# Banded attention heads as a pipeline in one fixed order, with smaller edits at the experts' start and end

## Chip, cores and metric

The kernel runs on one core of a Trainium2 chip. Its time is the device time of one execution, in microseconds (us). The program computes one layer of a diffusion backbone in one launch.

## What is computed

The reference, cut to the parts that the change touches:

```python
# banded heads: 8 query heads, 2 key/value heads, 512 tokens in 4 blocks of 128, 256 context tokens
s_loc = einsum('bnqkgd,bnjkd->bnkgqj', qbk, kband)     # own block and its neighbours
s_ctx = einsum('bnqkgd,bjkd->bnkgqj', qbk, k_ctx)
s_loc = where(|distance| <= 128 and in range, s_loc, -1e30)
p = softmax(concatenate([s_loc, s_ctx, sink_col], -1))  # sink_col: one learned number per head
o = einsum(p_loc, vband) + einsum(p_ctx, v_ctx)
x = x + g1 * (concatenate([ya, yb], -1) @ w_out)        # ya: four differential heads, yb: banded heads
hx2 = modulate(rmsnorm(x, norm2_g), sh2, sc2)
# 32 experts, each token goes to its top 4: h = xb @ w_gu[e] + b; clamped SwiGLU; a @ w_dn[e] + b
x = x + g2 * moe(hx2)
return rmsnorm(x, final_g)
```

## The kernel before

All products run on TensorE (PE). A float32 matrix is split into a high and a low part, and a product of two such matrices is three products (mm3). The stages in time are: the adaLN vectors, norms and projections; four differential heads (A); sixteen units of banded heads (B); the router; 31 experts' gate-up and down products as a pipeline; the last expert and the final norm.

A unit of the banded stage is a pair (n, m) of a block of 128 queries and a pair of heads; the loop at line 1171 goes over n and within it over m, 0 to 3. For each unit, scores_B (line 809) multiplies the queries of both heads with the keys: 512 keys where n is 0 or 3 and 640 where it is 1 or 2, cut in pieces of at most 512 columns. A piece is two products: the first on 128 rows (queries high and low against the high keys) and the second on the 64 rows of the low keys; then come masks of 128 columns. Both heads' scores lie in one PSUM tile "sc" of 1536 columns, the second from column 768. The first unit has two tiles of its own. One element per head is the sink, copied behind the scores by DVE for one head and by ACT for the other. DVE then takes both maxima (nmB), ACT both exponentials (pB, with their sums rsB), DVE the reciprocal, and DVE scales one head's pB and ACT the other's.

turn_B (870) transposes pB in groups of two key blocks for both heads (tiles "tp"), ACT copies them out as pTh and DVE takes the rest, pTl. mix_B (881) multiplies with the values into the tile "o", shared by two units. put_B (888), at odd m, adds the halves of o (yB, two copies on ACT and two adds on DVE) and splits the sum. out_proj (1040) does six products of 512 columns for one of eight row blocks of w_out; prep_out splits a part of w_out. Between units of block n stand the steps of block n - 1: norm2 (1057) at m = 0, route_T at 1, route at 2 (choice of the experts), rank at 3 (places in the experts' tables, with four indirect DMAs from POOL). router_vectors runs once.

The order of the work on each engine is a scheduler's, except where the list "pinned" names the engine: there instructions stay in the order of the program (the wrapper class at line 42, whose line 52 is the line of most rows). The banded stage isn't pinned. From line 1320 and in the experts' pipeline (1640) PE, DVE and ACT are.

In the experts' pipeline each unit is one block of 1024 weight columns or rows: unit_split (1565) splits it on ACT and DVE six units ahead of unit_products (1574). The list extra holds further steps by unit number: tables (1608) loads the four slot tables by DMAs on ACT's queue at unit 11, enter_rows adds them at unit 14. The last expert stands outside: down of expert 30 (1535), gate_up_last (1501), then its down product by the list "esq" and rows (1743), which puts results in place through the tiles p0, p1, y, h and tpm.

Of the kernel before, what the change touches and what calls it, by code (L numbers as in the profile page):

```python
# [10 lines left out]
F32 = mybir.dt.float32  # L11
# [14 lines left out]
KB = 8  # L26
# [11 lines left out]
def tile_block(ctx: ExitStack, tc: tile.TileContext, a: dict, out: bass.AP, dbg=None):  # L38
# [770 lines left out]
    def scores_B(n, m):  # L809

        b0, b1 = max(n - 1, 0), min(n + 2, 4)
        L = (b1 - b0) * 128
        nk = C + L
        g = m // 2
        rw = slice(g * 64, g * 64 + 64)
        q = qT[n]
        own = n + m < KN["own"]
        if own:
            assert nk == 512
            sv = [ps_pj() for _ in range(2)]  # L820
        else:
            s = sc_tile(KN["sB"])
            sv = [s[:, 0:TA], s[:, TA:2 * TA]]
        for i in range(2):
            hd, s = 2 * m + i, sv[i]
# [15 lines left out]
        nm = bp.tile([128, 2], F32, name="nmB", bufs=4)  # L841
        rs = bp.tile([128, 2], F32, name="rsB", bufs=4)
        w = nk if own else nk + 1
        for i in range(0 if own or KN["snk"] == "P" else 2):
            (V.tensor_copy if KN["snk"][i] == "V" else S.copy)(sv[i][:, nk:w], sinkB[:, 2 * m + i:2 * m + i + 1])
        for i in range(2):
            V.tensor_reduce(nm[:, i:i + 1], sv[i][:, 0:w], axis=AX.X, op=OP.max, negate=True)
        if own:
            es = bp.tile([128, 3, 2], F32, name="esB", bufs=1)
            V.tensor_scalar_mul(es[:, 0], sinkB[:, 2 * m:2 * m + 2], -1.0)  # L850
            V.tensor_tensor(nm, nm, es[:, 0], op=OP.min)
            V.tensor_add(es[:, 1], nm, sinkB[:, 2 * m:2 * m + 2])
            S.activation(es[:, 2], es[:, 1], AF.Exp)
        pp = []
        for i in range(2):
# [3 lines left out]
        if own:  # L859
            V.tensor_add(rs, rs, es[:, 2])  # L860
        V.reciprocal(rs, rs)
        for i in range(2):
            if KN["scB"][i] == "S":
                S.activation(pp[i][:, 0:nk], pp[i][:, 0:nk], AF.Copy, scale=rs[:, i:i + 1])
            else:
# [305 lines left out]
    for i, (n, m) in enumerate(units):  # L1171
# [4 lines left out]
        if m == 0 and n > 0:  # L1176
            start_Y(n)
# [674 lines left out]
```

## Time and profile before

| | |
|---|---|
| median of 3 runs | 1696.1 us (1688.65 to 1696.68) |
| the profiled execution | 1695.95 us, span 1694.2 us |
| TensorE's granted clock, mean | 0.965 |
| PE busy | 1609.1 us, 95% |
| DVE, ACT, POOL busy | 1482.8, 1093.7, 211.6 us |
| chain that ended last | PE 86%, DVE 5%, issue 4%, ACT 2%, DMA 2% |

Engines: PE is TensorE's products, PEld its weight loads, DVE VectorE, ACT ScalarE, POOL GpSimd, SP SyncE. PEclk is the granted clock, 1.00 or 0.50 at a time (2.4 or 1.2 GHz). A timeline row gives the start, the time that the instruction or its group took, and in brackets how long the engine had been idle and what released it.

### The profile page before, as it was taken

The numbers are of one execution on the slowest core, as the hardware profiler recorded it, in microseconds if no ns is written. First come the engines' busy times: TensorE is split into PE (matmuls) and PEld (weight loads), VectorE is DVE, ScalarE is ACT, GpSimd is POOL, SyncE is SP. The second block draws the span as 40 slices with busy tenths as digits, with TensorE's granted clock in tenths as the row PEclk, the third lists the DMA queues.
The fourth block names the chain that finished last, engine by engine and source line by source line (L and its number), as shares of the span: only waits on it lengthen the run. The fifth ranks groups of instructions, "written<-read, shape, count | busy, mean of one in ns | idle before, by whom it ended". The sixth has DMA issues, their size and how long they took to land.

```text
span 1694.2 us, 20948 instructions
## 1 busy us (share of the span) xinstructions
PE 1609.1 (95%) x7464; PEld 1286.3 (76%) x7464; DVE 1482.8 (88%) x1755; ACT 1093.7 (65%) x1406; POOL 211.6 (12%) x134
## 2 busy tenths in 40 slices
PE   7799997999888999999999999999999999999995
PEld 2687775677676888888888888888888888888873
DVE  6988797556777999999999999999999999999895
ACT  6544435445555776777776777776777776777763
POOL 0000001012331111111111111111111111111011
PEclk9999997788979999999999999999999999999998
DMA  9524325611569999999999999999999999999982
GB/s 350 174 85 131 107 88 162 169 49 40 193 234 345 352 359 367 362 361 379 376 362 364 366 365 378 382 363 367 366 363 381 374 362 367 361 369 365 363 274 91
DMA packets 115922, 494.11 MB, mean 292 GB/s; under 512 B 16641, under 2 KB 39338, under 8 KB 68642
## 3 DMA queue, kind: packets, MB, share of 16 engines
q1 hardware_dynamic: 99090, 456.44, 70.6%
q0 software_dynamic: 14128, 28.91, 8.2%
q10 hardware_dynamic: 2592, 7.34, 1.2%
q8 instruction: 61, 1.00, 0.2%
q14 instruction: 51, 0.42, 0.1%
HBM read 472.91 MB, written 27.57 MB: 295 GB/s over the span
## 4 chain that ended last, share of the span: by engine, by line
PE 86%; DVE 5%; issue 4%; ACT 2%; DMA 2%; POOL 0%; ACTq 0%; SPq 0%; DVEq 0%; POOLq 0%
PE h L52 41%; PE y L52 21%; PE pj L52 10%; PE sc L52 5%; PE tpm L52 3%; PE tp L52 3%; PE o L52 2%; DVE wp L52 1%; DVE two L52 1%; DMA ys<-slot_d 1%; PE g L52 1%; DMA w<-in_w_mod_dram 1%; PE p L52 0%; ACT wp L52 0%; ACT pB L52 0%
## 5 line engine op out<-in xcount | busy, mean ns | idle before, releaser
L52 PE MATMUL h<-two 128*128 128x512 f32 x1666 | 415.1, 400 | 1.4 <-DVE two L52 1.4
L52 PEld LDWEIGHTS h<-two 128*128 128x128 f32 x1666 | 310.1, 189 | 72.1 <-DVE two L52 2.2
L52 PE MATMUL h<-wp,two 128*128 128x512 f32 x1314 | 328.5, 400 | 4.1 <-DVE pk L52 4.1
L52 DVE TENSOR_TENSOR two<-wp,two 128x1024 fp32r<-128x1024 f32 x254 | 301.1, 1219 | 8.0 <-ACT two L52 7.9
L52 PEld LDWEIGHTS h<-wp,two 128*128 128x128 f32 x1314 | 244.4, 190 | 57.4 <-ACT two L52 4.3
L52 ACT CAST two<-wp 128x1024 fp32r<-128x1024 f32 x254 | 257.8, 1049 | 16.4 <-PE y L52 13.1
L52 DVE TENSOR_TENSOR wp<-wp 128x1024 fp32r<-128x1024 f32 x176 | 205.4, 1218 | 2.7 <-ACT wp L52 2.7
L52 DVE TENSOR_TENSOR two<-w,two 128x1024 fp32r<-128x1024 f32 x170 | 200.1, 1218 | 2.3 <-ACT two L52 2.3
L52 POOL DMA_INDIRECT acc<-ys,slot_i x31 | 103.7, 3345 | 705.4 <-DVE ys L52 705.4
L52 ACT CAST wp<-wp 128x1024 fp32r<-128x1024 f32 x176 | 176.1, 1050 | 12.8 <-PE y L52 7.7
L52 ACT CAST two<-w 128x1024 fp32r<-128x1024 f32 x170 | 170.4, 1049 | 16.6 <-PE y L52 11.9
L52 PE MATMUL y<-two,ah 128*128 128x512 f32 x540 | 169.4, 395 | 0.0
L52 PE MATMUL y<-wp,ah 128*128 128x512 f32 x452 | 142.8, 397 | 0.0
L52 DVE TENSOR_TENSOR wp<-w,wp 128x1024 fp32r<-128x1024 f32 x104 | 125.5, 1218 | 7.2 <-ACT wp L52 7.1
L52 ACT CAST wp<-w 128x1024 fp32r<-128x1024 f32 x104 | 108.8, 1049 | 27.6 <-PE pj L52 10.3
L52 PEld LDWEIGHTS y<-two,ah 128*128 128x128 f32 x540 | 101.3, 188 | 24.4
L52 ACT CAST ah<-tpm 128x512 fp32r<-128x512 f32 x64 | 37.5, 588 | 127.3 <-PE tpm L52 127.3
L52 PE MATMUL y<-two,al 128*128 128x512 f32 x270 | 106.7, 395 | 0.0
L52 PEld LDWEIGHTS y<-wp,ah 128*128 128x128 f32 x452 | 85.8, 190 | 20.7 <-ACT ah L52 0.4
L52 DVE TENSOR_TENSOR wp<-wchunk,wp 128x1024 fp32r<-128x1024 f32 x82 | 98.3, 1218 | 0.0
L52 PE MATMUL pj<-xh,wp 128*128 128x512 f32 (+1 forms) x320 | 91.7, 364 | 1.9 <-ACT xf L52 1.0
L52 PE MATMUL y<-wp,al 128*128 128x512 f32 x226 | 90.0, 398 | 2.1 <-DVE al L52 2.1
(343 smaller groups left out, 2401.0 us busy)
## 6 DMA issues: line engine op xcount, KB each, us to landing
wp<-in_w_gate_up_dram SPq DMA_DIRECT2D x139, 1024.0 KB
w<-in_w_gate_up_dram SPq DMA_DIRECT2D x87, 1024.0 KB
wp<-in_w_down_dram SPq DMA_DIRECT2D x76, 1024.0 KB
w<-in_w_down_dram SPq DMA_DIRECT2D x41, 1024.0 KB
wchunk<-in_w_gate_up_dram SPq DMA_DIRECT2D x30, 1024.0 KB
wm<-in_w_mod_dram SPq DMA_DIRECT2D x64, 256.0 KB
wchunk<-in_w_down_dram SPq DMA_DIRECT2D x11, 1024.0 KB
w<-in_w_in_dram SPq DMA_DIRECT2D x14, 512.0 KB
```

The costliest lines, as they stand in the source:

```text
L52: i = f(*args, **kwargs)
```

## The change

The function scores_B becomes a class, Scores, with one call per head for the scores and the maximum and one for the exponential. The loop's instructions on PE, DVE and ACT stay in program order, in which the next unit's two heads stand between this unit's transposes. The probabilities are no longer scaled: put_B multiplies the finished sums by the reciprocals, which PE transposes. The sink element is written by a product on PE. The low keys are copied to tiles of 128 rows, the other 64 of them zero. The slot tables are loaded at unit 4 instead of 11, two of them by GpSimd's queue, and added at unit 16 instead of 14 by one reduction. The last expert's two halves and the down product of expert 30 are units of the pipeline. Some buffers are shared or made fewer (pB 5 to 4, lg 2 to 1, fill and zt in one). In the tail, p0 and p1 become halves of the tile y, and two of the tiles of rows halves of h.

The diff, cut:

```diff
+    klB = bp.tile([128, 2, TA], F32R, name="klB")
+    for g in range(2):
+        rw, ro = slice(g * 64, g * 64 + 64), slice(64 - g * 64, 128 - g * 64)
+        G.memset(klB[ro, g].bitcast(F32), 0.0)
+        S.copy(klB[rw, g], kB[rw, 2].bitcast(F32))
+    class Scores:
...
+        def __init__(self, n, m):
+            self.n, self.m = n, m
+            self.b0, b1 = max(n - 1, 0), min(n + 2, 4)
+            self.blocks = [4, 5] + list(range(self.b0, b1))
+            self.nk = len(self.blocks) * 128
+            self.own = n + m == 0
+            if self.own:
+                self.sv = [ps_pj() for _ in range(2)]
+            else:
+                s = sc_tile(KN["sB"])
+                self.sv = [s[:, 0:TA], s[:, TA:2 * TA]]
+            self.w = self.nk if self.own else self.nk + 1
+            self.nm = bp.tile([128, 2], F32, name="nmB", bufs=4)
+            if m % 2 == 0:
+                sums[n, m // 2] = bp.tile([128, 4], F32, name="rsB", bufs=3)
+            self.rs = sums[n, m // 2][:, m % 2 * 2:m % 2 * 2 + 2]
+            self.pp = []
...
+        def head(self, i):
+            n, m, nk, s = self.n, self.m, self.nk, self.sv[i]
+            hd, g, q = 2 * m + i, m // 2, qT[n]
             cuts = [(0, C), (C, nk)] if i == 1 or nk == 512 else [(0, C), (C, 512), (512, nk)]
-            masks = []
-            if n > 0:
-                masks.append((mprev, C))
-            if n < 3:
-                masks.append((mnext, nk - 128))
-            ksl = lambda x0, x1: slice(T + x0, T + x1) if x0 < C else slice(b0 * 128 + x0 - C, b0 * 128 + x1 - C)
+            masks = ([(mprev, C)] if n > 0 else []) + ([(mnext, nk - 128)] if n < 3 else [])
+            ksl = lambda x0, x1: slice(T + x0, T + x1) if x0 < C else slice(self.b0 * 128 + x0 - C, self.b0 * 128 + x1 - C)
             for x0, x1 in cuts:
                 PE.matmul(s[:, x0:x1], q[:, hd], kB[:, g, ksl(x0, x1)], start=True, stop=False)
                 mk = [(mt_, y) for mt_, y in masks if x0 <= y < x1]
-                PE.matmul(s[:, x0:x1], q[rw, hd], kB[rw, 2, ksl(x0, x1)], start=False, stop=not mk)
+                PE.matmul(s[:, x0:x1], q[:, hd], klB[:, g, ksl(x0, x1)], start=False, stop=not mk)
                 for j, (mt_, y) in enumerate(mk):
                     PE.matmul(s[:, y:y + 128], identb, mt_, start=False, stop=j == len(mk) - 1)
-            if not own and KN["snk"] == "P":
+            if not self.own:
                 PE.matmul(s[:, nk:nk + 1], ones3, sink3[:, hd:hd + 1], start=True, stop=True)
...
-        pp = []
-        for i in range(2):
-            p = bp.tile([128, 641], F32, name="pB", bufs=5)
-            S.activation(p[:, 0:w], sv[i][:, 0:w], AF.Exp, bias=nm[:, i:i + 1], accum_out=rs[:, i:i + 1])
-            pp.append(p)
-        if own:
-            V.tensor_add(rs, rs, es[:, 2])
-        V.reciprocal(rs, rs)
-        for i in range(2):
-            if KN["scB"][i] == "S":
-                S.activation(pp[i][:, 0:nk], pp[i][:, 0:nk], AF.Copy, scale=rs[:, i:i + 1])
-            else:
-                (V if KN["scB"][i] == "V" else G).tensor_scalar(pp[i][:, 0:nk], pp[i][:, 0:nk], rs[:, i:i + 1], 1.0,
-                                                             op0=OP.mult, op1=OP.mult)
-        return pp, [4, 5] + list(range(b0, b1))
+            V.tensor_reduce(self.nm[:, i:i + 1], s[:, 0:self.w], axis=AX.X, op=OP.max, negate=True)
+        def sinks(self):
+            self.es = bp.tile([128, 3, 2], F32, name="esB", bufs=1)
+            V.tensor_scalar_mul(self.es[:, 0], sinkB[:, 2 * self.m:2 * self.m + 2], -1.0)
+            V.tensor_tensor(self.nm, self.nm, self.es[:, 0], op=OP.min)
+            V.tensor_add(self.es[:, 1], self.nm, sinkB[:, 2 * self.m:2 * self.m + 2])
+            S.activation(self.es[:, 2], self.es[:, 1], AF.Exp)
+        def exp(self, i):
+            p = bp.tile([128, 641], F32, name="pB", bufs=4)
+            S.activation(p[:, 0:self.w], self.sv[i][:, 0:self.w], AF.Exp, bias=self.nm[:, i:i + 1], accum_out=self.rs[:, i:i + 1])
+            self.pp.append(p)
+    sums = {}
...
-    def put_B(g, o, y):
+    def put_B(n, g, o, y):
 
         ov = o.rearrange("p (j q) -> p j q", j=4)
         yb = bp.tile([128, 2, 128], F32, name="yB", bufs=1)
+        rs = sums[n, g]
+        V.reciprocal(rs, rs)
+        rb = ps_tp()
+        for j in range(4):
+            PE.transpose(rb[:, j, :], rs[:, j:j + 1].to_broadcast([128, 128]), ident)
         S.copy(yb[0:64], ov[64:128, 0::2, :])
         S.copy(yb[64:128], ov[0:64, 1::2, :])
         V.tensor_add(yb[0:64], ov[0:64, 0::2, :], yb[0:64])
         V.tensor_add(yb[64:128], ov[64:128, 1::2, :], yb[64:128])
+        V.tensor_mul(yb[0:64], yb[0:64], rb[0:64, 0::2])
+        V.tensor_mul(yb[64:128], yb[64:128], rb[64:128, 1::2])
         fb = slice(4 + 2 * g, 6 + 2 * g)
...
-    cur = scores_B(0, 0)
+    cur = Scores(0, 0)
+    for i in range(2):
+        cur.head(i)
+    cur.sinks()
+    for i in range(2):
+        cur.exp(i)
+    V.tensor_add(cur.rs, cur.rs, cur.es[:, 2])
...
+    def norm2_factor(t):
+        t1, ss, late = rt[t]
         rs = lp.tile([128, 1], F32, name="rs2", bufs=2)
-        S.activation(sq, x1[t], AF.Square, accum_out=ss)
...
+    pinned[0] = "PVS"
     for i, (n, m) in enumerate(units):
-        nxt = scores_B(*units[i + 1]) if i < 15 else None
+        nxt = Scores(*units[i + 1]) if i < 15 else None
         if m % 2 == 0:
             o = ps_o()
-        pp, blocks = cur
-        if m == 0 and n > 0:
-            start_Y(n)
-        if n == 0 and m == KN["ys"][0]:
-            start_Y(n, slice(0, KN["yh"]))
-        if n == 0 and m == KN["ys"][1]:
-            start_Y(n, slice(KN["yh"], 4))
+        pp, blocks = cur.pp, cur.blocks
         fill = [(n - 1, 6), (n - 1, 7)] if m == 0 else [(n, 2 * m - 2), (n, 2 * m - 1)]
-        if n == 0:
-            fill = [(0, kb) for kb in KN["f0"][m]]
+        if n + m == 0:
+            fill = []
         bls = [list(range(x, min(x + 2, len(blocks)))) for x in range(0, len(blocks), 2)]
-        pts = [turn_B(pp, bl) for bl in bls[:2]]
-        for k, bl in enumerate(bls):
-            if k == 2:
-                pts.append(turn_B(pp, bl))
-            if k < len(fill):
-                out_proj(fill[k][0], [fill[k][1]])
-            mix_B(m, pts[k], bl, blocks, o)
-        cur = nxt
-        if m % 2 == 1:
-            put_B(m // 2, o, Yt[n][1])
+        pts = []
+        for k in range(2):
+            if nxt:
+                nxt.head(k)
+            pts.append(turn_B(pp, bls[k]))
+            if nxt:
+                nxt.exp(k)
+        if m == 0:
+            start_Y(n, slice(0, 4 if n else 3))
+        if (n, m) == (0, 2):
+            start_Y(n, slice(3, 4))
         if n == 0 and m < 3:
             prep_out(2 * m + 2)
             prep_out(2 * m + 3)
-        if n == 0 and m == 2:
+        if m == 1 and n > 0:
+            norm2_factor(n - 1)
+        for f in fill[0:1]:
+            out_proj(f[0], [f[1]])
+        mix_B(m, pts[0], bls[0], blocks, o)
+        if len(bls) > 2:
+            pts.append(turn_B(pp, bls[2]))
+        for f in fill[1:2]:
+            out_proj(f[0], [f[1]])
+        for k in range(1, len(bls)):
+            mix_B(m, pts[k], bls[k], blocks, o)
+        if m % 2 == 1:
+            put_B(n, m // 2, o, Yt[n][1])
+        cur = nxt
+        if (n, m) == (0, 2):
             router_vectors()
...
+    tabs = gp.tile([128, 4, E, 3], F32, name="tabs")
...
+        elif b.half is not None:
+            c0 = b.half * 1024
+            if i == 0:
+                if b.half == 0:
+                    lasth.append(psH.tile([128, 2048], F32, name="h", bufs=1))
+                b.ps = lasth[0]
+                open_h(e, b.ps[:, c0:c0 + 1024], c0)
+            (xh_, xl_), kb = xg[e], i
...
-    tabs = []
     def tables():
 
-        st = mt.tile([128, D], F32, name="ys", bufs=1)[:, 0:9 * E].rearrange("p (k e w) -> p k e w", k=3, w=3)
-        tabs.extend([slot_t] + [st[:, k] for k in range(3)])
         for k in range(4):
-            S.dma_start(tabs[k], slot_d[k][E:129 * E].rearrange("(p e) w -> p e w", e=E))
+            (S, G)[k // 2].dma_start(tabs[:, k], slot_d[k][E:129 * E].rearrange("(p e) w -> p e w", e=E))
 
     def enter_rows():
-        slot_rows(slot_t, tabs[1:], slot_i)
+        V.tensor_reduce(slot_t, tabs.rearrange("p k e w -> p e w k"), axis=AX.X, op=OP.add)
+        slot_rows(slot_t, (), slot_i)
+    lasth = []
...
-            for u, f in ((3, turn_last_gates), (5, lambda: start_acc(3, ps_tpm)), (7, count), (8, leave_front), (11, tables), (14, enter_rows)):
+            for u, f in ((3, turn_last_gates), (5, lambda: start_acc(3, ps_tpm)), (7, count), (8, leave_front), (4, tables), (16, enter_rows)):
...
+    halves = [Block(last, False, hf) for hf in range(2)]
+    for b in (halves[0], Block(last - 1, True), halves[1]):
+        units += [(b, i) for i in range(8)]
+    for k in range(2):
+        extra.setdefault(u0 + (2, 4)[k], []).append(turn(last - 1)[k])
...
+    steps0 = []
+    extra.setdefault(u0 + 8, []).append(lambda: (steps0.append(activation(last, lasth[0][:, 0:1024], 0, 1)), next(steps0[0])))
+    for k in range(3):
+        extra.setdefault(u0 + 8 + k, []).append(lambda: next(steps0[0]))
+    extra.setdefault(u0 + 16, []).append(lambda b=units[u0 + 8][0]: add_rows(last - 1, b.ps))
+    extra.setdefault(u0 + 18, []).append(lambda: turn(last)[0]())
...
+    yl = psm.tile([128, D], F32, name="y", bufs=1)
+    py = [yl[:, n * 512:(n + 1) * 512] for n in range(2)]
...
+            x = psH.tile([128, 2048], F32, name="h", bufs=1)
+            for t in range(2):
+                pt[t, 0], pt[t, 1] = x[:, t * D:t * D + 512], x[:, t * D + 512:t * D + D]
...
+        pt[3, n] = py[n]
```

## Rows read from the trace of the kernel before

**Rows 1.** Stretches: length, busy us (instructions) of each engine, PEclk, DMA share, GB/s

```profile
305.00:461.00 156.00, 144.09 (x719) 111.71 (x719) 94.84 (x227) 75.32 (x174) 30.80 (x29) 0.87 0.35 110
...
345.00:348.50 3.50, 1.79 (x13) 1.34 (x12) 2.63 (x6) 3.45 (x9) 0.00 (x0) 0.96 0.35 131
...
348.70:359.00 10.30, 10.30 (x32) 7.37 (x31) 3.63 (x7) 2.63 (x7) 0.90 (x1) 0.50 0.27 51
...
505.00:552.00 47.00, 39.61 (x167) 31.53 (x166) 35.91 (x43) 27.19 (x30) 5.62 (x4) 0.93 0.91 348
...
552.00:1606.00 1054.00, 1054.00 (x4758) 862.54 (x4757) 1004.64 (x927) 772.26 (x842) 135.25 (x56) 1.00 0.98 367
...
1621.90:1625.30 3.40, 3.40 (x8) 2.75 (x9) 3.40 (x4) 3.11 (x4) 0.00 (x0) 0.50 1.03 243
```

**Rows 2.** Timeline of one unit: start, us, engine, instruction; in brackets idle before, releaser

```profile
437.64 1.04 PE L52 MATMUL tp<-ident,pB 128*128 128x128 f32 x8
...
438.44 1.30 PE L52 MATMUL sc<-kB,qB 128*128 128x256 f32 x4
...
441.94 1.28 DVE L52 TENSOR_REDUCE nmB<-sc 128x1 f32<-128x513 f32 x2
...
443.31 0.69 ACT L52 ACTIVATE pB<-sc,nmB 128x513 f32<-128x513 f32 x1 [1.75 <-DVE nmB L52]
...
444.99 0.72 ACT L52 ACTIVATE pB<-pB,rsB 128x512 f32<-128x512 f32 x1 [0.23 <-DVE rsB L52]
445.00 0.49 DVE L52 TENSOR_SCALAR pB<-pB,rsB 128x512 f32<-128x512 f32 x1
```

**Rows 3.** Timeline at the first scores of unit (1,0)

```profile
317.38 0.21 ACT L52 ACTIVATION_READ_ACCUMULATOR pB<-sc,nmB 128x1 f32 x1
...
317.65 0.69 PE L52 MATMUL sc<-kB,qB 128*128 128x256 f32 x2 [0.48 <-ACT pB L52]
```

**Rows 4.** Timeline: two products of one mix

```profile
453.24 0.28 PE L52 MATMUL o<-pTh,vB 128*128 128x256 f32 x1
...
453.35 0.28 PE L52 MATMUL o<-pTl,vB 128*128 128x256 f32 x1
```

**Rows 5.** PE groups by shape, 305 to 461: busy, mean ns, idle before

```profile
L52 PE MATMUL sc<-kB,qB 64*128 64x256 f32 x44 | 18.5, 421 | 0.0
```

**Rows 6.** DVE and ACT groups by shape, 305 to 461, as in the group above

```profile
L52 DVE TENSOR_REDUCE nmB<-sc 128x1 f32<-128x641 f32 x16 | 12.4, 818 | 0.7 <-ACT sc L52 0.7
...
L52 DVE TENSOR_TENSOR yB<-o,yB 64x256 f32<-64x256 f32 x16 | 6.8, 422 | 7.9 <-ACT yB L52 7.6
...
L52 DVE TENSOR_TENSOR t<-pj,g1B 128x512 f32<-128x512 f32 x6 | 4.2, 692 | 2.4 <-PE pj L52 2.4
...
L52 DVE SCALAR_TENSOR_TENSOR t<-t,rs,sh2B 128x1024 f32<-128x1024 f32 x3 | 3.9, 1284 | 1.6 <-PE tp L52 1.6
L52 DVE TENSOR_TENSOR two<-yB,two 128x256 fp32r<-128x256 f32 x7 | 3.5, 493 | 0.0
...
L52 ACT ACTIVATE pB<-sc,nmB 128x641 f32<-128x641 f32 x16 | 12.7, 798 | 4.3 <-DVE nmB L52 3.7 <-PE tp L52 0.5
...
L52 ACT COPY yB<-o 64x256 f32<-64x256 f32 x16 | 5.9, 367 | 7.5 <-PE o L52 7.3
```

**Rows 7.** Timeline ahead of the slow clock at 348.7

```profile
348.05 0.36 PE L52 MATMUL o<-pTh,vB 128*128 128x256 f32 x1 [1.34 <-DVE yB L52]
```

**Rows 8.** Timeline on the way into the experts

```profile
508.16 0.34 ACTq L52 DMA_DIRECT2D slot_t<-slot_d  x1
...
529.46 1.42 PE L52 MATMUL h<-two 128*128 128x512 f32 x5 [1.43 <-DVE two L52]
...
544.77 1.10 PE L52 MATMUL tpm<-ident,g 128*128 128x128 f32 x4 [5.96 <-issue]
```

**Rows 9.** DVE groups by line, 505 to 530

```profile
L52 DVE TENSOR_TENSOR slot_t<-slot_t,ys 128x96 f32<-128x96 f32 x3 | 0.8, 258 | 6.5 <-DMA ys<-slot_d 6.5
```

**Rows 10.** Timeline in the tail

```profile
1621.90 0.80 PE L52 MATMUL y<-wp,al 128*128 128x512 f32 x1 [2.07 <-DVE al L52]
```

More of the change, by code (lines that the diff above doesn't have):

```diff
@@ L842, in scores_B @@
[L842 to L845, printed above, removed]
-        for i in range(2):
[L847 to L853, printed above, removed]
@@ L1001, in tile_block @@
     V.memset(zrow, 0.0)
-    Gt = lp.tile([128, E], F32, name="Gt")
     g3 = lp.tile([128, 3, E], F32R, name="g3")
@@ L1012, in tile_block @@
     slot_d = [dr.tile([(T + 1) * E, 3], F32, name=f"slot{k}_d") for k in range(4)]
-    fill = lp.tile([128, E * 3], F32, name="fill")
-    V.memset(fill, 0.0)
+    zt = lp.tile([128, 4, 128], F32, name="hT", bufs=1).rearrange("p a b -> p (a b)")
+    V.memset(zt, 0.0)
+    fill = zt[:, 0:E * 3]
     for k in range(4):
@@ L1064, in norm2 @@
         ss = lp.tile([128, 1], F32, name="ss2", bufs=2)
+        S.activation(sq, x1[t], AF.Square, accum_out=ss)
+        rt[t] = t1, ss, late
+    def norm2_factor(t):
+        t1, ss, late = rt[t]
         rs = lp.tile([128, 1], F32, name="rs2", bufs=2)
-        S.activation(sq, x1[t], AF.Square, accum_out=ss)
         rstd_of(rs, ss, D)
@@ L1097, in choose @@
         rs = rt[t][1]
-        lg = lp.tile([128, E], F32, name="lg", bufs=2)
+        lg = lp.tile([128, E], F32, name="lg", bufs=1)
         V.scalar_tensor_tensor(lg, pl, rs, brB, op0=OP.mult, op1=OP.add)
@@ L1212, in tile_block @@
             load_qB(n + 2)
+    pinned[0] = ""
     most = mo.tile([1, 1], I32, name="most")
@@ L1555, in tile_block, with __init__ @@
     class Block:
-        def __init__(self, e, down):
-            self.e, self.down, self.ws = e, down, None
+        def __init__(self, e, down, half=None):
+            self.e, self.down, self.half, self.ws = e, down, half, None
         def load(self):
             if self.ws is None:
-                self.ws = gu0 if self.e == 0 and not self.down else (load_dn(w_dn[self.e]) if self.down else load_gu(w_gu[self.e]))
+                if self.down:
+                    self.ws = load_dn(w_dn[self.e])
+                elif self.half is not None:
+                    self.ws = load_half(w_gu[self.e], self.half)
+                else:
+                    self.ws = gu0 if self.e == 0 else load_gu(w_gu[self.e])
     def unit_split(u):
@@ L1567, in unit_split @@
         b.load()
-        if b.down:
+        if b.down or b.half is not None:
             return msplit(b.ws[i])
@@ L1639, in tile_block, with last_slots @@
             at(24).append(lambda e=e - 1, b=units[u0 + 16][0]: add_rows(e, b.ps))
+    u0 = len(units)
+    halves = [Block(last, False, hf) for hf in range(2)]
[3 more added lines that the diff above has]
+        extra.setdefault(u0 + (2, 4)[k], []).append(turn(last - 1)[k])
+    ohT = None
+    def last_slots():
+        nonlocal ohT
+        ohT = xg_tiles(("t",))[0][0][:, 0:4]
+        tk = mt.tile([128, 4], F32, name="tk")
+        V.tensor_scalar(tk, dumr[:, 3:7], slot_t[:, last, 0:1], dumr[:, 0:1], op0=OP.add, op1=OP.add)
+        for t in range(4):
+            V.tensor_scalar(ohT[:, t], iotaS, tk[:, t:t + 1], None, op0=OP.is_equal)
+    extra.setdefault(u0 + 6, []).append(last_slots)
+    steps0 = []
[4 more added lines that the diff above has]
+    extra.setdefault(u0 + 18, []).append(lambda: turn(last)[0]())
     pinned[0] = "PVS"
@@ L1652, in tile_block @@
     pinned[0] = ""
-    ohT, ys = xg_tiles(("t",))[0][0][:, 0:4], xrow[0]
-    tk = mt.tile([128, 4], F32, name="tk")
-    V.tensor_scalar(tk, dumr[:, 3:7], slot_t[:, last, 0:1], dumr[:, 0:1], op0=OP.add, op1=OP.add)
-    for t in range(4):
-        V.tensor_scalar(ohT[:, t], iotaS, tk[:, t:t + 1], None, op0=OP.is_equal)
-    ws = load_dn(w_dn[last - 1])
-    for f in turn(last - 1):
-        f()
-    down(last - 1, ws, slot_t[:, last - 1, 1:2], slot_i[:, last - 1:last])
-    psH_es.close()
-    psT = psT_es.enter_context(tc.tile_pool(name="psT", bufs=1, space=PSUM))
-    h_last = gate_up_last(last, w_gu[last])
+    ys = xrow[0]
     def load_rows():
@@ L1694, in tile_block @@
     fgB, xo = load_rows()
-    st = turn(last)
-    st[0]()
-    py = [psT.tile([128, 512], F32, name=f"p{n}") for n in range(2)]
+    yl = psm.tile([128, D], F32, name="y", bufs=1)
+    py = [yl[:, n * 512:(n + 1) * 512] for n in range(2)]
     ah, al = actT[last]
@@ L1713, in part @@
             wsp[kb] = wsp[kb][:, 0], wsp[kb][:, 1]
-    glu_steps = activation(last, h_last[:, 0:1024], 1, 1)
+    glu_steps = activation(last, lasth[0][:, 1024:2048], 1, 1)
     yp = None
```

47 lines of the change are left out of this document (4 added, 43 removed).

## Prediction

> **What bounds the kernel now.** I read the stretches first [rows 1]. From 552 to 1606 us the PE is busy for all 1054.00 us at granted clock 1.00: the experts' products are the bound there, and no edit before or behind can shorten them. What can move is the banded stage (305 to 461), the way into the experts (461 to 552) and the tail (from 1606). In the banded stage the PE is busy 144.09 of 156 us, yet DVE only 94.84 and ACT 75.32, and the clock is 0.87, not 1. A clock that is either 1 or 0.5 and has a mean of 0.87 was at 0.5 for 26% of 156 us, 40.6 us; that cost half of it, 20.3 us. So the stage is 144.1 - 20.3 = 123.8 us of PE work at full clock, 20 us of slow clock and 12 us of idle PE.
>
> Next, the order within one unit [rows 2]. The score products run from 438.44 in 1.30 us for four, the second head's behind the first's; both maxima stand together at 441.94; the exponentials start only when both are over (443.31, after 1.75 us of waiting for the maxima), and at 444.99 and 445.00 come the two scalings. Elsewhere the next unit's scores start 0.06 us after the second exponential's accumulator was read (317.38 + 0.21 to 317.65) and the row names the exponential as what the PE waited for [rows 3]. I read from this that the score tile of both heads is one object for the waits: any write to it waits for every earlier reader, of either head. The PE hid that so far, since its order isn't pinned here and out_proj and mix products were free to stand in between.
>
> **The change part by part.**
>
> Low keys on 128 rows. Four 256-column score products, alternately 128 and 64 rows high, take 1.30 us [rows 2], 0.31 apart, while 256-column products all 128 rows high start 0.12 apart (453.24, 453.35) [rows 4]. The stage has 44 pairs of 256 columns [rows 5], and by the cuts in the code 8 pairs of 384 and 8 of 128. The first save 88 x 0.19 = 16.7; for the others I scale by columns: 16 x 0.19 = 3.0 and 16 x 0.13 = 2.1. Sum: 21.8 us of PE work. The two zero fills and copies for it are made once (some 4 us of POOL and ACT, beside head A's work): nothing, or up to 2 if they land in front of the first scores.
>
> Sinks by TensorE and division behind the values. Gone are 15 one-column copies on DVE and 15 on ACT between the scores and the maxima, and per unit a reciprocal and one scaling on each of DVE (0.49) and ACT (0.72) [rows 2]. Added: 30 one-column products (no row shows one of this kind; 0.04 to 0.11 each, between a third of a 256-column step and a transpose; I take 0.11: 3.3 us), and in each of 8 put_B four transposes of 0.11 (eight take 1.04 with the last one's tail [rows 2]; 3.5 us), a reciprocal and two DVE products (0.42 each, as the yB adds) [rows 6]. DVE gets 15 x 0.49 = 7 lighter (the copies apart) and 8 x 0.84 = 7 heavier: about even. ACT loses 15 x 0.72 = 11 us, but it wasn't the bound.
>
> So the PE has, with the scores of two units that before lay ahead of 305 (2 us): 123.8 - 21.8 + 3.3 + 3.5 + 2 = 110.8 us of work, 13 less.
>
> The fixed order. Now PE, DVE and ACT each run the unit's steps as written: head 0, four transposes, exponential 0, head 1, four transposes, exponential 1, then out_proj, mix, put_B. By the one-object reading head 1's scores wait for exponential 0. Behind head 0's last product come the maximum (0.82), the exponential (0.80 + 0.20) and hand-overs of 0.06 to 0.1 each, 2.2 us together [rows 3, 6], and the PE has only four transposes, 0.45, to run meanwhile; ACT first copies out these transposes, beside the maximum. Exposed: 1.7 us per unit with 640 keys, 1.4 with 512: 8 x 1.7 + 7 x 1.4 = 23 us. Behind head 1 out_proj and mix follow, 2 x 1.4 + 8 x 0.12 at least, so the second exponential is hidden.
>
> What DVE and ACT must finish before the next maximum, since it stands behind in their queues:
> - put_B (8 times): from the last mix the two ACT copies, two adds, two products, the split's two steps, 0.74 + 0.84 + 0.84 + 2 x 0.49 = 3.4 [rows 6], then the next maximum. The PE has head 0's scores and four transposes, 1.2. About 2 us each beyond the 1.7 already counted: 16 us.
> - norm2 at m = 0 (n = 1 to 3): four DVE steps of 0.69, and on ACT a Square ahead of an exponential: 3 x 3 = 9 us.
> - route and rank at m = 2, 3: t (1.28) and the small steps of the choice and of rank, in my estimate 3 us more: three times, 13 us, of which I count 10, as some lie beside mix.
> - router vectors, once: some steps of the size of t, 3 us.
> Sum 38 us; its ends are 10 (DVE has 60 us to spare in the stage, and much of this could lie beside out_proj) and 50.
>
> The clock. In 345.0 to 348.5 it is granted at 0.96 and the PE is busy 1.79 of 3.50 us; from 348.7 it stands at 0.50 for 10.3 us, in which the PE is never idle [rows 1]. The wait ahead of it is 1.34 us for put_B's adds [rows 7]. After the change such waits stand in nearly every unit. Before, the slow clock cost 20.3 of 144 us; I take 13 for 111 us of work; ends 0 and 30.
> The Trainium skill ("TensorE: Matmul & The Clock Gate", A second HAM failure mode: psum-queue depth-cycling) tells of a kernel whose PE idles briefly between groups of products often enough that the clock swings between its two levels; it speaks against this change, and the trace agrees by the 10.3 us named. By it alone the cost lies at my upper end, 30 us, and the forecast at 1727.
>
> Start: units no longer stand between head A's last steps, which so end a few us earlier; I take 302 for the loop's start, three before the window of the stage. End of the stage: 302 + 111 + 23 + 38 + 13 = 487, against 461: **26 us later**. Ends: 302 + 111 + 23 + 10 + 0 = 446 and 302 + 111 + 23 + 50 + 30 = 516.
>
> Early tables. Now ACT issues the slot tables from 508.16 [rows 8]; DVE waits three times for them, 6.5 us together [rows 9], and what it splits comes late: the PE idles 1.43 us at 529.46 and 5.96 before 544.77 [rows 8]. The PE is busy 39.61 of 47 us at clock 0.93 in 505 to 552 [rows 1], so at most 7.4 idle and 47 x 0.07 = 3.3 of slow clock can be won, 10 together. Issued seven units (about 10 us) earlier, half of them on GpSimd's queue, where only a fill and later gathers stand behind, the tables land before they are asked for. I take -8, ends -3 and -10; and 0 if the rank's last writes land too late.
>
> Units to the end. The PE waits 2.07 us for al at 1621.90 [rows 10] and then runs 3.4 us at half clock (1.7 lost) [rows 1]; as units the last experts' activations stand between other products and both go: -3.8. But py and pt become halves of one tile each: by the same reading the output's first half waits for the second's products, +1 to +2 (eight products of 0.23, and a scaling of about 0.7 as other steps on 512 columns [rows 6]). I take -2, ends -5 and +2.
>
> Sum: 26 - 8 - 2 = +16 on the profiled run's 1695.95, which is 0.15 below the median: **1712 us**. Its own range, with ends added half-way, is 1698 to 1735.
>
> **Rivals.**
> *Faster: the queues give way.* If a unit's waits lie beside out_proj and mix, because two heads' halves can be used apart, and the clock holds, the 13 us of PE work and the 12 us of idle go as intended: 302 + 111 + 12 + 10 + 5 = 440, 21 earlier; with the tables and the tail 1695.95 - 21 - 10 = 1665; with half of the 23 us exposed 1677. For it speaks that DVE and ACT have 60 and 80 us to spare; against it rows 3 and the order of rows 2. It decides where head 1's scores start before exponential 0 ends. I put it at 1672.
> The Trainium skill ("PSUM — Partial Sum Buffer", PSUM bank collisions raise a hardware error) asks only that two engines don't touch one bank at once; by it halves in different banks could go in parallel, but the second head starts at column 768, in the middle of a bank, so by that rule too the first products would have to wait. No run here shows it.
> *No change: half the queue waits.* With 19 us of queue waits and 10 of slow clock the stage ends at 465 + some us of late start, up to 471: +10, and tables and tail give it back: 1696.
>
> **How the numbers follow.** A kernel of this length repeats within some 0.5%, 8.5 us, which is the bound of no change. Slower as summed: 0.50 (1698 to 1735). No change: 0.20 (1688 to 1704). Faster: 0.30 (1660 to 1687). The likeliest is 1712. The range takes in most of the faster case: 1664 to 1735. Of the chances, faster 0.30, same 0.20, slower 0.50.
>
> **What would show it.** Right: the PE waits for an exponential before head 1 of each unit; the maxima stand apart, each behind its own head; the granted clock in the stage is under 0.87; the stage ends near 487; no DVE wait for the slot tables; no 2 us wait for al. Wrong: head 1's scores run while exponential 0 does; the clock stays at 1; or out_proj covers the waits at put_B, so that the stage ends before 455.

## Result and the profile after

The changed kernel takes 1740.25 us (1738.32 to 1741.14, 4 runs) against 1694.32: a ratio of 1.0279, 95% interval 1.0252 to 1.0307. It was forecast slower, by 16 us; it is 46 us slower, outside the range given. The profiled execution has a span of 1739.1 us, 44.9 more than before.

All of the loss lies in the banded stage. From the first transposes of unit (0,0) to the last mix it lasts 152.0 us before and 217.7 after; it starts 10.9 us earlier and ends 54.8 later. First the stretch before, then after, then after the steady experts, which answer to [rows 1]: length, busy us (instructions) of PE, PEld, DVE, ACT, POOL, granted clock, DMA share, GB/s.

```profile
307.20:459.20 152.00, 143.30 (x714) 111.04 (x712) 93.06 (x220) 74.53 (x171) 28.71 (x27) 0.87 0.35 108
```

```profile
296.30:514.00 217.70, 148.53 (x803) 127.09 (x802) 100.53 (x204) 72.83 (x157) 28.00 (x27) 0.77 0.29 89
600.00:1640.00 1040.00, 1040.00 (x4696) 851.13 (x4695) 994.69 (x919) 761.88 (x831) 135.35 (x56) 1.00 0.98 367
```

The PE's idle time goes from 152.00 - 143.30 = 8.7 us to 217.70 - 148.53 = 69.2. The mean clock falls from 0.87 to 0.77; for a clock that is 1 or 0.50 that means 2 x 0.23 x 217.7 = some 100 us at the lower level (40 before). Summed over the stretches at 0.50 in the clock's record, the PE is busy 68.7 us there, which costs half, 34 us (19.6 before). What is left, 148.5 - 34.3 = 114.2 us, is the PE's work at full clock (123.7 before). So the work shrank by 9.5 us, and waits and clock took 60 and 15 more. (The split is good to a few us: kernels below with the same products come out at 113 to 119 us of such work.) DVE is busy 100.53 and ACT 72.83 of the 217.7 us, so neither is full either.

What the PE waits for in the stage after (engine, group, releaser: us in total, times, longest):

```profile
PE sc L52 <- ACT pB L52: 50.0, 15, 5.1
...
PE tp L52 <- DVE yB L52: 8.4, 5, 1.8
...
PE tp L52 <- DVE rsB L52: 7.5, 1, 7.5
```

Fifteen units, fifteen waits of a score product for an exponential, 50.0 us, where the same group had 1.5 us in three waits before:

```profile
PE sc L52 <- ACT pB L52: 1.5, 3, 0.8
```

How one of the fifteen comes about is seen in the order of time, at the scores of unit (2,1):

```profile
405.43 0.19 DVE L52 TENSOR_TENSOR pos<-tp,selb 128x32 f32<-128x32 f32 x1
...
407.04 0.37 DVE L52 TENSOR_REDUCE lg<-eq 128x32 f32<-128x128 f32 x1
...
407.66 0.19 DVE L52 TENSOR_TENSOR g<-lg,g 128x32 fp32r<-128x32 f32 x1
407.77 0.82 DVE L52 TENSOR_REDUCE nmB<-sc 128x1 f32<-128x641 f32 x1
...
408.62 0.80 ACT L52 ACTIVATE pB<-sc,nmB 128x641 f32<-128x641 f32 x1 [2.66 <-DVE nmB L52]
409.31 0.19 ACT L52 ACTIVATION_READ_ACCUMULATOR pB<-sc,nmB 128x1 f32 x1
...
409.56 0.58 PE L52 MATMUL sc<-kB,qB 128*128 128x256 f32 x1 [4.28 <-ACT pB L52]
```

The scores of head 0 were ready at 403.3. Their maximum starts only at 407.77, since DVE has first to run put_B's last step and the thirteen small steps of rank (405.43 to 407.85). Then the exponential, 0.80, and its accumulator, 0.19; 0.06 us later the PE starts head 1's scores, having stood 4.28 us.

One wait is of another kind, in unit (0,1):

```profile
313.56 0.56 SPq L911 DMA_DIRECT2D wo<-in_w_out_dram  x1
...
320.01 1.04 ACT L52 CAST wp<-wo 128x1024 fp32r<-128x1024 f32 x1 [6.18 <-DMA wo<-in_w_out_dram]
321.09 1.23 DVE L52 TENSOR_TENSOR wp<-wo,wp 128x1024 fp32r<-128x1024 f32 x1 [7.22 <-ACT wp L52]
...
323.77 0.17 DVE L52 RECIPROCAL rsB<-rsB 128x4 f32<-128x4 f32 x1
...
324.09 1.09 PE L52 MATMUL tp<-ident,rsB 128*128 128x128 f32 x4 [7.50 <-DVE rsB L52]
```

A row block of w_out was asked for at 313.56 and came 6.4 us later; ACT stood for it, DVE behind ACT, and put_B's reciprocal and transposes behind both, so the PE stood 7.50 us. In a free order put_B need not have stood behind it.

Behind the stage the change wins: of the 54.8 us at the end of the stage 50.6 are left at the experts' first down product and 44.9 at the end. DVE no longer waits for the slot tables [rows 9]: the addition has no idle time ahead of it.

```profile
L52 DVE TENSOR_REDUCE slot_t<-tabs 128x96 f32<-128x384 f32 x1 | 0.9, 870 | 0.0
```

### The profile page after: what moved, and what is told of

It is laid out like the page before. It is cut to its first block, busy times and chain, and to the rows that moved or that the text cites. A ratio compares the mean times of both kernels' runs of the same rounds, so it can differ in the third digit from the quotient of the medians.

```text
span 1739.1 us, 21064 instructions
## 1 busy us (share of the span) xinstructions
PE 1600.9 (92%) x7526; PEld 1293.8 (74%) x7526; DVE 1482.1 (85%) x1729; ACT 1084.3 (62%) x1377; POOL 215.1 (12%) x138
## 3 DMA queue, kind: packets, MB, share of 16 engines
q1 hardware_dynamic: 99218, 456.44, 68.7%
## 5 line engine op out<-in xcount | busy, mean ns | idle before, releaser
L52 PE MATMUL h<-two 128*128 128x512 f32 x1694 | 421.5, 399 | 3.0 <-ACT two L52 3.0
L52 PEld LDWEIGHTS h<-two 128*128 128x128 f32 x1694 | 314.8, 189 | 74.8 <-ACT two L52 3.9
L52 PE MATMUL h<-wp,two 128*128 128x512 f32 x1338 | 335.3, 400 | 4.1 <-DVE hT L52 4.1
L52 PEld LDWEIGHTS h<-wp,two 128*128 128x128 f32 x1338 | 249.4, 190 | 58.5 <-ACT two L52 4.3
L52 ACT CAST two<-wp 128x1024 fp32r<-128x1024 f32 x254 | 258.1, 1049 | 16.9 <-PE y L52 14.6
L52 PE MATMUL y<-two,ah 128*128 128x512 f32 x556 | 174.5, 395 | 0.8 <-DVE w L52 0.8
L52 PE MATMUL y<-wp,ah 128*128 128x512 f32 x468 | 147.1, 395 | 0.4 <-DVE wp L52 0.4
L52 ACT CAST wp<-w 128x1024 fp32r<-128x1024 f32 x104 | 108.7, 1050 | 23.4 <-PE pj L52 10.3
```

The lines of the kernel that those rows point to most:

```text
L52: i = f(*args, **kwargs)
```

## Experiments

Each time stands beside the kernel before on the same chip (medians 1691.6 to 1693.6), as a ratio with its 95% interval. "Stage" is always from the first transposes of unit (0,0) to the last mix. The expectations name three theories. T: the PE stands inside each unit because the second head's scores wait for the first head's readers of the shared score tile. Q: DVE's and ACT's fixed queues alone delay each maximum, which stands behind put_B, norm2, route and rank. W: the new work itself (division, sinks, low keys) is slow. D, later, is a DMA at the head of a fixed queue.

**The order taken away.** One line of the changed kernel, "pinned" around the loop, says which engines keep the program's order:

```diff
-    pinned[0] = "PVS"
+    pinned[0] = ""
     for i, (n, m) in enumerate(units):
```

> The changed kernel with the banded loop not pinned on any engine; the work is that of the changed kernel. T and Q: the stage is no longer than before the change (154 us) less some of the 9 us of PE work now missing, so with tables and units to the end (about -10) 1670 to 1690. W: 1710 or more.

1665.56 us, ratio 0.9845 (0.9797 to 0.9892): the same work in the scheduler's order is 27 us faster than before, a little more than expected, and 75 faster than in the fixed order. T and Q both stand; W, that the new work itself is slow, falls as the cause of the 46 us, and so do the smaller buffers, which this run has too.

With only the PE, and with only DVE and ACT kept in order ("P", "VS"):

> The changed kernel with only TensorE kept in program order in the banded loop; DVE and ACT are ordered by the scheduler. T: the second head's scores still stand behind the first exponential, some 1.7 to 2.5 us in 15 units, but not behind put_B's or norm2's steps: PE waits for ACT pB 25 to 35 us, 1705 to 1720. Q: the waits go, 1675 to 1690.

> The changed kernel with DVE and ACT kept in program order in the banded loop and TensorE not. T: TensorE can put out_proj and mix into the wait for the first exponential: PE waits for ACT pB under 25 us, 1695 to 1710. Q: the DVE and ACT queues still delay each maximum, 1725 or more.

"P" took 1700.15 us (ratio 1.0044, 1.0018 to 1.007), "VS" 1708.11 (1.0097, 1.0063 to 1.0131). The first lies between T's and Q's ranges. Either alone costs 35 to 43 us over the free order, both 75. With "P" the PE's waits for the exponential are 30.0 us, 2.0 per unit, which is what T had for the shared tile (1.7 and 1.4); with DVE and ACT released the other 20 are gone. With "VS" they are 0.4, since out_proj and mix can step in; yet it is the slower of the two: T had 1695 to 1710 there, but its waits now stand elsewhere, in front of the values' products and put_B's transposes.

```profile
PE sc L52 <- ACT pB L52: 30.0, 15, 3.0
```

```profile
PE o L52 <- DVE pTl L52: 14.7, 13, 3.0
...
PE tp L52 <- DVE yB L52: 10.1, 7, 2.3
...
PE tp L52 <- DVE rsB L52: 7.8, 1, 7.8
...
PE sc L52 <- ACT pB L52: 0.4, 1, 0.4
```

**The shared score tile.** First I moved both heads of the next unit ahead of the transposes, each still with its maximum:

```diff
         for k in range(2):
             if nxt:
                 nxt.head(k)
+        for k in range(2):
             pts.append(turn_B(pp, bls[k]))
+        for k in range(2):
             if nxt:
                 nxt.exp(k)
```

> The changed kernel with one thing moved: in the fixed order both heads' scores (and maxima) of the next unit stand ahead of this unit's transposes, and both exponentials behind them; no product or wait is taken away. Theory T (the PE stands in each unit before the second head's scores, which wait for the first exponential because both heads share one score tile): PE waits for ACT pB fall from 50 us to under 15, the stage from 220 us to some 170 to 180, the time from 1740 to 1690 to 1705. Theory Q (the fixed DVE and ACT queues alone: maxima and copies behind put_B, norm2, route, rank): the maxima still stand behind the same steps, so the waits only move; 1725 or more. Theory W (the changed work itself: division, sinks, 128-row low keys): no change, 1740.

1731.42 us (1.0249, 1.02 to 1.0298), only 9 us better by the medians and 5 by the ratios. My expectation was wrong, and the waits show why: the score product now waits for the maximum of head 0, 41.3 us in 14 waits. The maximum, too, reads the tile, and it stands in DVE's queue behind put_B and the rest.

```profile
PE sc L52 <- DVE nmB L52: 41.3, 14, 5.4
```

So the products of both heads have to stand ahead of both maxima, as before the change (nxt.most is the maximum, taken out of head):

```diff
-        for k in range(2):
-            if nxt:
-                nxt.head(k)
-            pts.append(turn_B(pp, bls[k]))
-            if nxt:
-                nxt.exp(k)
+        for f in (nxt.head, nxt.most) if nxt else ():
+            for k in range(2):
+                f(k)
+        for k in range(2):
+            pts.append(turn_B(pp, bls[k]))
+        for k in range(2):
+            if nxt:
+                nxt.exp(k)
```

> The changed kernel, still in one fixed order, in which the products of both heads of the next unit stand ahead of both maxima, then this unit's transposes, then both exponentials. Within a unit no product waits any more for a reader of the score tile; only the next unit's first product does, behind the second exponential. Theory T (the shared score tile inside the unit is most of the PE's wait): PE waits in front of score products fall from 50 us (41 in the run with heads moved) to under 15, the stage from 200 to 155 to 165, the time to 1680 to 1695. Theory Q (the fixed DVE and ACT queues: a maximum stands behind put_B, norm2 and rank): the wait goes over to the next unit's transposes or first product, 30 us or more remain, 1700 to 1715.

1696.24 us (1.0015, 0.9995 to 1.0034): 44 us better than the change, by this order alone, with all three engines still fixed. 35 of it lie between this run and the one before, which differ in the place of the maxima alone. No score product waits any more; the stage has 169.5 us with 38.0 idle and a clock of 0.89.

```profile
298.50:468.00 169.50, 131.48 (x797) 111.04 (x796) 97.16 (x203) 70.78 (x157) 28.05 (x27) 0.89 0.36 111
```

```profile
PE tp L52 <- DVE rsB L52: 12.0, 1, 12.0
...
PE o L52 <- DVE pTl L52: 10.2, 11, 2.2
...
PE o L52 <- ACT pTh L52: 6.9, 6, 2.1
PE tp L52 <- DVE yB L52: 6.3, 5, 1.8
```

The time lies between T's and Q's ranges: the tile was the larger part, the queues keep the rest.

**A DMA at the head of a fixed queue.** The 12.0 us that the PE waits once for the reciprocal in that run are the wait for w_out (ACT stands 9.8 us for it, DVE 11.1 behind ACT). Its splitting was put one unit later, in the changed kernel and in the last one:

```diff
-        if n == 0 and m < 3:
-            prep_out(2 * m + 2)
-            prep_out(2 * m + 3)
+        if n == 0 and m > 0:
+            prep_out(2 * m)
+            prep_out(2 * m + 1)
```

> The changed kernel with the splitting of w_out's row blocks 2 to 7 one unit later in the program (it is used one unit after that). In the changed kernel ACT stands 6.18 us at 320.01 for a block of w_out that was issued at 313.56, and put_B's reciprocal and transposes stand behind it in the fixed order, PE 7.50 us. Theory D (a DMA at the head of a fixed queue): that wait goes, -6 to -12, 1728 to 1734. Rival: the next reader (the queue waits of the units behind) takes it over, 1738 or more.

> The fixed order with both heads' products ahead of the maxima (1696) and w_out's blocks split one unit later. D: its PE wait of 12.0 us for put_B's reciprocal goes: 1682 to 1688. Rival: 1692 or more. What then is left over the free order (1666) is the price of the fixed DVE and ACT queues alone.

1733.18 us (1.0237, 1.0182 to 1.0292) and 1690.04 (0.9985, 0.9963 to 1.0007): 7 and 6 us won, within D's range in the first and 2 us short of it in the second. The intervals overlap with those of the two kernels without the edit, so the times alone would not show it; the PE's waits do: the one for the reciprocal is down to 1.2 and 1.9 us. In the second a new one of 4.3 us stands where router_vectors (brB) holds a slot. It is the same kind again: ACT stands 5.62 us for another block of w_out, and brB's addition is behind that in DVE's queue.

**What the fixed queues still cost.** Some 24 us lie between the last run and the free order.

> The fixed order with both heads' products first and w_out's blocks later (1690), but only TensorE kept in program order; DVE and ACT free. If the DVE and ACT queues make the rest (theory Q): near the free order, 1666 to 1674. If PE's own order does: 1684 or more.

> The same with DVE and ACT kept in program order and TensorE free. Theory Q: stays at 1684 or more, since every maximum and copy still stands behind the steps ahead of it. If PE's order makes the rest: 1666 to 1674.

> The same with all three engines fixed, and norm2, route_T, route, rank, turn_gates and start_acc put off: they stand behind the next unit's scores, maxima, transposes and exponentials in the program instead of ahead of them; put_B stays. The prediction put 22 us of queue waits on these steps. If they make the rest: 1668 to 1678. If put_B and the short chains of copies do: 1684 or more.

With only the PE fixed 1669.96 us (0.9891, 0.9867 to 0.9915), with only DVE and ACT fixed 1686.83 (0.9972, 0.9952 to 0.9991). So some 16 to 21 of the 24 us are the price of the DVE and ACT order, what is left of the waits for w_out included; the PE's own order, once the tile's readers are out of its way, costs 4 to 8. (The ends are by the ratios and by the medians.) Here are the stages of the two, with the free order first:

```profile
302.20:440.10 137.90, 122.99 (x792) 104.29 (x790) 89.20 (x198) 64.47 (x146) 29.59 (x27) 0.97 0.39 124
```

```profile
304.90:444.10 139.20, 123.86 (x798) 106.54 (x796) 90.17 (x201) 64.88 (x151) 28.57 (x27) 0.95 0.37 117
```

```profile
293.90:458.20 164.30, 133.86 (x797) 113.14 (x796) 98.32 (x204) 70.72 (x158) 28.19 (x27) 0.90 0.37 122
```

Putting norm2, route and rank off behind the next unit's exponentials was no remedy: 1704.65 us (1.01, 1.0076 to 1.0125), at least 15 worse. The edit collects their calls in a list and runs it behind the exponentials:

```diff
+        while pend:
+            pend.pop(0)()
...
-            (norm2, route_T, route, rank)[m](n - 1)
+            pend.append(lambda n=n, m=m: (norm2, route_T, route, rank)[m](n - 1))
```

Their transposes and products on the PE now stand behind this unit's transposes, and need a "tp" slot that DVE has not yet read out: 17.4 us in 10 waits, which the kernel without the edit didn't have. So this run does not say what the steps cost where they stood; it says that this other place costs more.

```profile
PE tp L52 <- DVE pTl L52: 17.4, 10, 2.4
```

**The parts, one by one, in the kernel before** (its order free).

> The kernel before with the low keys on 128 rows alone (and the smaller buffers that make room: pB 4, fill and zt in hT's slot, lg 1). By the prediction 21.8 us less PE work in the stage; if the PE bounds the unpinned stage, 1672 to 1680. Rival: the stage's chains of scores, maxima, exponentials and transposes take over, and at most 8 us are won: 1686 to 1692.

```diff
-                PE.matmul(s[:, x0:x1], q[rw, hd], kB[rw, 2, ksl(x0, x1)], start=False, stop=not mk)
+                PE.matmul(s[:, x0:x1], q[:, hd], klB[:, g, ksl(x0, x1)], start=False, stop=not mk)
```

1665.37 us, ratio 0.985 (0.9816 to 0.9883): 28 us by the medians and 25 by the ratio, more than the 14 to 22 that I expected. The profiles are 32.6 us apart: the stage lasts 124.0 us instead of 152.0 and starts 4.6 earlier. The score products of a group now start 0.11 to 0.12 apart, against 0.31 [rows 2]; only behind the first of a group it is 0.20 in the median.

```profile
399.86 0.28 PE L52 MATMUL sc<-klB,qB 128*128 128x256 f32 x1
...
399.97 0.28 PE L52 MATMUL sc<-kB,qB 128*128 128x256 f32 x1
...
400.09 0.28 PE L52 MATMUL sc<-klB,qB 128*128 128x256 f32 x1
```

```profile
302.60:426.60 124.00, 109.15 (x714) 92.71 (x712) 92.92 (x219) 75.11 (x173) 28.21 (x27) 1.00 0.41 127
```

By the same sum as above the work at full clock is 109.1 us, 14.6 less than before; and the granted clock is 1.00 throughout, so that the 19.6 us of slow clock are gone as well; idle time is 14.9 instead of 8.7. 14.6 + 19.6 - 6.2 = 28.

> The kernel before with the edits behind the banded loop alone: slot tables at unit 4 on two queues and entered at 16, the last expert's halves and the down product of expert 30 as pipeline units, the tail's tiles. By the prediction's terms (-8 and -2) 1684; by the difference of the two profiles behind the banded stage (54 us later at its end, 45 at the end of the span) 1685. Rival: these edits only took up time that the later stage end had left for weights to land, then within 4 us of 1694.

(Edit: the part of the change's diff behind the loop.) 1680.58 us, 0.9918 (0.9888 to 0.9947): 13 us. From the last mix to the first down product the profile has 83.1 us instead of 93.1, so 10 in front of the experts, and 5.7 us less behind it, where the PE's wait for al [rows 10] is gone.

> The kernel before with the division behind the values alone (no scalings of pB; reciprocals transposed by the PE and multiplied in put_B). By the prediction about even, 1690 to 1698. Rival: the chain scores, maximum, exponential, reciprocal, scaling, transposes is shorter by 1 us in each unit and the stage follows it: 1680 to 1688. Other rival: put_B's longer chain delays out_proj: 1700 or more.

(Edit: the reciprocal and the scalings go, put_B as in the change.) 1707.07 us, 1.0097 (1.0059 to 1.0135): 13 slower, as in the second rival. But put_B's longer chain is a small part of it at most: the transposes of the reciprocals wait for nothing, as their row says.

```profile
308.90:472.10 163.20, 151.80 (x746) 118.53 (x744) 91.78 (x210) 65.29 (x157) 28.51 (x27) 0.85 0.33 104
```

```profile
L52 PE MATMUL tp<-ident,rsB 128*128 128x128 f32 x32 | 5.9, 308 | 0.0
```

The stage is 11.2 us longer; the PE is busy 8.5 us more (5.1 of work at full clock, the transposes, and 3.4 of slow clock) and idle 2.7 more (11.4). DVE and ACT have less to do (91.78 and 65.29 against 93.06 and 74.53), and it buys nothing. In the free order the stage follows the PE, and here the PE got more work, at a clock of 0.85.

> The kernel before with the sinks by TensorE alone (30 one-column products in place of 15 copies on DVE and 15 on ACT). One product of this kind took 0.17 to 0.21 us in the trace of the changed kernel. By the prediction 3 us of PE work more, and the copies' hand-overs fewer (0.16 each, between scores and maxima): -4 to +3, 1690 to 1697. Rival: the copies with their waits (ACT 20 us for the DVE copy in the trace of before) held up the chain, 1684 or less.

```diff
-'snk': 'VS'
+'snk': 'P'
```

1702.12 us, 1.0051 (1.0021 to 1.008): 9 to 11 slower, above my range. The PE is idle 9.4 us and busy 155.0; at 0.50 it is busy 59.2 us of it (39.1 before). So 10 of the 12 us by which the stage is longer are slow clock and 1.7 are work. Why the clock fell more here I can't say; the run shows only that it did.

```profile
308.00:472.40 164.40, 155.03 (x740) 119.92 (x738) 94.18 (x208) 72.96 (x158) 28.24 (x27) 0.82 0.32 99
```

**What beats both.** Low keys and the edits behind the loop, nothing else of the change:

> The kernel before with two parts of the change alone: the low keys on 128 rows (with the smaller buffers) and the edits behind the banded loop (early tables, units to the end); no fixed order, no division behind the values, no sinks by TensorE. If the two gains (-28 and -13 as measured apart) add, 1650 to 1655, faster than every kernel so far. Rival: both gains are partly the same (an earlier start of the experts that waits for the same weights), 1658 to 1665.

1653.9 us (1650.9 to 1657.24), ratio 0.9777 (0.9727 to 0.9828). The two gains nearly add: 28 + 13 = 41, measured 38. Its stage is that of the low keys alone, 124.5 us at clock 1.00.

```profile
302.80:427.30 124.50, 109.15 (x714) 92.71 (x712) 92.83 (x220) 75.04 (x173) 28.32 (x27) 1.00 0.42 127
```

Division and sinks, which cost 13 and 9 alone, cost 12 together on top of this kernel: the change in the free order, which has all four parts, takes 1665.56.

## Why the prediction was wrong in size

**What bounds the stage.** The PE and its waits, as said. What I didn't see: the 20 us of slow clock before went when the 64-row products went, though idle time grew (below).

**PE work.** 110.8 us predicted, 114.2 measured. The saving of the low keys was put at 21.8; alone it came to 14.6 by the busy time at full clock, so this term was too large by a third; a part of that is the first product of each group, which did not come down to 0.12. (Its pieces of 384 and 128 columns are not scaled by columns as it says; that would give 4.6 and 1.5 in place of 3.0 and 2.1.) The clock it gives back, another 19.6 us in the free order, had no term at all. The sinks' price (3.3) was too high, about 1.5 by the starts of the products (last section). The transposes' (3.5) was in the right place and too low, 5.1 alone. The division's other price I weighed on DVE, "about even", though DVE did not bound the stage; alone it cost 13 us.

**The waits of the fixed order.** 23 + 38 = 61 us predicted, 69.2 measured. The mechanism, head 1's scores behind exponential 0, stands: 15 waits, 50.0 us, and 30.0 with only the PE fixed, against 23. The list behind the 38 was half right. DVE and ACT in order add 20 in those waits, as in the rows around rank above, 8.4 for slots that put_B's factors (yB) hold, and 7.5 for w_out, which the list didn't have: I had named no DMA that stands at the head of a fixed queue. That norm2, route and rank make 22 of it wasn't shown, and moving them didn't win it back.

**The clock.** This is the step that failed: 13 us taken, 34 measured, beyond even the end of 30 that I gave. I scaled the loss of before to less work. The part of it that belonged to 64-row products should have gone, and the part that waits make should have grown with them: the stage has 69 us of idle time, 50 of it in 15 gaps of 1.4 to 5.1 us, and some 100 of its 218 us are at the lower level. In kernels with the same products the slow clock grows with the idle time, though not in step: it costs 4.0 us at 14.9 idle (free order), 13.4 at 38.0 (both heads' products first), 21.2 at 35.0 (first run with only the PE fixed) and 34.3 at 69.2.

What the Trainium skill tells ("TensorE: Matmul & The Clock Gate", A second HAM failure mode: psum-queue depth-cycling) of a PE that idles briefly between groups of products is borne out by the change: a wait in every unit, and a clock of 0.77. With its upper end of 30 the prediction's sum gives 1729, not the 1727 that it states; either is nearer than 1712. Idle time alone does not decide, though: the kernel with low keys on 128 rows is idle 12% of its stage and holds 1.00, the kernel before is idle 6% and has 0.87. So the 10.3 us at 0.50 before, which the prediction counts as agreement, do not show what waits cost.

**Start.** 302 predicted, 296.3 measured. Sum: 296.3 + 114.2 + 34.3 + 69.2 = 514.0, against 302 + 111 + 13 + 61 = 487: minus 6, plus 3, plus 21 and plus 8 make the 27 us between the two; tables and tail won the 10 that were taken. The range was wrong in its sum, too: ends half-way to the bounds given make 1689 to 1731, not 1698 to 1735; 1740 lies outside either.

**Tables and tail.** -8 and -2 predicted. In the changed kernel the way from the last mix to the first down product is 4.1 us shorter and the rest of the program 5.7; alone, in the kernel before, it was 10.0 and 5.7. So the sum of 10 came out with both parts off, by luck. That halves of one tile hold the tail up, put at 1 to 2 us, shows in every trace: from the first scaling of the last expert's output (oh) to the end are 23.7 us in all runs with this edit and 21.0 to 21.3 in those without. The halves of y share no column, yet in the changed kernel a product into the second waits for DVE's addition that reads the first:

```profile
1719.06 0.69 DVE L52 TENSOR_TENSOR w<-w,y 128x512 f32<-128x512 f32 x1 [1.50 <-PE y L52]
...
1719.81 0.73 PE L52 MATMUL y<-two,ah 128*128 128x512 f32 x2 [0.78 <-DVE w L52]
```

**Rivals.** "Faster: the queues give way" has nearly the right price, but for another kernel: in the free order the same work takes 1666, against its 1672, and the stage ends at 440.1, against its 440. That is partly luck: the PE has 119 us of work there, not 111, and 19 of idle time and slow clock, not 27. The point that I named, whether head 1's scores start before exponential 0 ends, decided it: in the fixed order they never do. The rule of the Trainium skill cited there ("PSUM — Partial Sum Buffer", PSUM bank collisions raise a hardware error) wasn't put to a test. The one-object reading was tested: a product into one head's columns waits for the other head's exponential (50.0 us), or for its maximum where that comes last (41.3), and in the tail one half of y waits for a reader of the other. Whether the whole tile is the unit or a part of it, no run tells. Two heads' products written before either maximum remove the wait without a second tile.

## What to carry to other kernels

A fixed program order turns every wait of one engine into a wait of all that is written behind it; before pinning a loop, look for each shared tile which readers stand between two writes, the short ones on the busiest queue too, and for each DMA whose landing the queue's head may have to wait for. Cost the parts of a bundle one by one: here two of its parts won 38 us and two others cost 13 and 9 in the same free order (12 together, with the first two in place), while the order put on top cost 75. Relieving engines that are not the bound bought nothing here, and giving their work to the one that is cost more than the work, since the clock moved with it: 5.1 us of work made the stage 11.2 longer, and 1.7 made it 12.4.

## Hardware

Unexpected was how the clock goes with the shape of the products. In the kernel before, with score products alternately 128 and 64 rows high, the PE runs 41.0 of 152 us at the lower level; in three kernels that keep the 64-row products and the free order it is the same or more (stage clock 0.85, 0.85 and 0.82). With 128-row products and the free order it is 1.00, 1.00 and 0.97, though the PE is busy 94% of the stage before and 88% in the low keys' kernel. The alternating products start 0.31 us apart at 1.00 and 0.51 at 0.50; among 128-row products 0.12. Whether it is the rows that move the clock, or the distance of the starts, the runs can't tell apart.

A one-column product is longer than its column, but holds up the next product little. In the changed kernel its mean from start to end is 191 ns; where nothing is waited for, the next product starts 30 ns after its own start at 1.00 and 72 to 73 at 0.50, while transposes of 128 columns start 110 ns apart at 1.00. The price of 0.11 us each in the prediction was a transpose's.

```profile
L52 PE MATMUL sc<-sink,ones 96*128 96x1 bf16 x30 | 5.7, 191 | 0.0
```

```profile
419.86 0.17 PE L52 MATMUL sc<-sink,ones 96*128 96x1 bf16 x1
...
419.89 0.63 PE L52 MATMUL tp<-ident,pB 128*128 128x128 f32 x4
```
